# Head projections of a retention layer as one queued software pipeline of steps

## The chip, the cores and the metric

The kernel runs on one core of a Trainium2 chip. Five engines work side by side, each through its own queue of instructions in order: TensorE (PE, matrix multiplication, with a second row PEld for its weight loads), VectorE (DVE), ScalarE (ACT), GpSimd (POOL) and SyncE (SP), which here only issues transfers. Engines wait for each other through semaphores. Data lies in DRAM, in on-chip tiles of 128 partitions (SBUF), or in eight PSUM banks of 128 x 512 fp32, where TensorE adds up its products. The metric is the device time of one execution in microseconds, the median of the runs.

## What is computed

A trunk of two layers over 512 tokens of width 2048, in fp32. The first layer mixes tokens by retention with 8 heads, the second by latent attention with 16 heads; both are modulated by a vector `c` (shift, scale, gate).

```
for i in range(2):
    mod = (silu(c) @ ada_w[i] + ada_b[i])[:, None, :]     # ada_w[i]: 2048 x 6144
    shift, scale, gate = jnp.split(mod, 3, axis=-1)
    h = rmsnorm(x, norm_g[i]) * (1.0 + scale) + shift
    y = retention_branch(h, ...) if i == 0 else mla_branch(h, ...)
    x = x + gate * y
return rmsnorm(x, final_norm_g)

def retention_branch(h, pos, w_in, gn_g, w_out):
    proj = h @ w_in                                       # 2048 x 12288
    q, k, v, g = jnp.split(proj, [2048, 4096, 8192], axis=-1)
    q, k = rope(q, pos), rope(k, pos) / 16                # 8 heads of 256
    y = chunkwise_retention(q, k, v)                      # v, g: 8 heads of 512
    y = (y - mean(y)) * rsqrt(var(y) + EPS) * gn_g        # per head
    return (silu(g) * y) @ w_out
```

## The kernel before

*Numbers.* Matrices are kept as a high and a low half in TensorE's format fp32r, and each product is three matmuls (`mm3`, L158: high with high, high with low, low with high). A weight block arrives raw (fp32, 128 x 1024, 512 KB) through SP's queue, `load_w` (L138); `split` (L133) makes its halves: ACT copies the high half (L134), DVE subtracts to get the low one (L135). Raw tiles and halves rotate through three buffers each (tags `raw`, `whi`, `wlo`). Scratch tiles of 128 x 512 have the tag `tmp`, with six buffers. PSUM is two groups of four banks, `acc` and `aux`.

*Order.* The program is traced once in Python. A scheduler in the framework then sets the order on each engine, from its own estimate of when each instruction could start; `tc.issue_after(x)` tells it to place what is traced inside behind instruction x. DMA issues stand in the queue of the engine that issues them.

*Stages.* First the input is normalised and the first layer's modulation is computed from streamed rows (`first_modulation`), woven with head 0's q, k, v and most of its gates (0 to about 183 us); then the last gate block of head 0 (`g03`), and from 205 us head 1's queries and keys. The rotary tables `cos`, `sin` are made by `rotary_tables` with DVE in this first stage and stay on chip until the retention of the last heads.

The stage that the change rewrites runs over heads h = 1 to 7 (loop at its end):

- `queries_and_keys(h, ...)`, for h up to 5: eight units, each a weight block of two k-tiles, 24 matmuls of 128x128 by 128x512 (`qk_raw`, `qk_hi`, `qk_lo`); at the end the four banks are copied by ACT into `st` tiles and stored by POOL (`keep_rows`, L489).
- `values_and_gates(h)` (L603): v and g of a head with seven products in place of eight for each 2 x 2 block (a Strassen-Winograd form). `form_sums` makes the sums of the activations once, next to head 1's queries and keys. First half: eight units, each with two raw blocks e and o (`vg_e_w`, `vg_o_w`); DVE forms three sums of weights (L639 and the lines after it), both blocks are split (the low half at L627), and 24 matmuls go to the banks x, s, y, z. At the turn (L660 to L666) ACT copies x, s and z away to scratch (m1, m5, m4), and DVE adds m1 to y and y, m5 to s in PSUM. Second half: eight units of blocks p (128 x 1024) and q (128 x 512), one sum, both split (L671 for p's copy), 18 matmuls to x, y, s; the products of y and s are held one unit back at the start. At the end x and s go out by `keep_rows`, and m4 + y, m5 + y by DVE and POOL.
- Beside this the other modulation rows come in: six pieces of 16 rows of 512 KB, each row loaded by SP into `mod_aw` (two buffers, tag `bw`) and added by DVE into `mod_am` with a factor of `c` (`later_modulation`, L500, L512/L514). Two rows go with each unit of queries and keys from head 2 on, one with every other unit of the second half of values and gates (`qk_each`, `vg_each`). `use_modulation` (L519) sums a finished piece over the partitions with a few small matmuls and adds the bias; for a gate piece the bias is fetched by POOL into `mod_brow`, and the result is stored by POOL.

Then the tile pool `lp` is closed, and in the next one, `l1`, heads 6 and 7's queries and keys are computed, woven with the retention of heads 0 and 1 (`retention`, with `rope_halves` for the rotation); `hooks` says at which unit a generator of a head is advanced by one part. The part of a head before its first `yield` fetches and rotates q and k and fetches v; the next computes scores. Then follow the other heads' retention within the output projection (`o`), and the second layer.

Of the kernel before, what the change touches and what calls it, by code (L numbers as in the profile page):

```python
# [16 lines left out]
P = 128  # L17
# [32 lines left out]
def hybrid_trunk_kernel(  # L50
# [222 lines left out]
    def rot(name):  # L273
        return base.tile([P, T], F32, tag="rot", bufs=2, name=name)
# [81 lines left out]
    cos, sin = rot("cos"), rot("sin")  # L356
    tables = rotary_tables(cos, sin, 0, False, "ret")
# [98 lines left out]
    for u in range(KD // 2):  # L456
# [4 lines left out]
        if u + 1 < KD // 2:  # L461
            am = first_modulation(u + 1, (there, u))
        else:
            first_load(there, u)
            for _ in tables:
                pass
        for kind in (here, "g"):
            for kt in (2 * u, 2 * u + 1):
                in_order(lambda: products(kind, kt))
# [19 lines left out]
    def keep_rows(ps, dst_d, r0, name, func=AF.Identity, own=None):  # L489

        st = lpp.tile([P, T], F32, tag="st", bufs=4, name=name) if own is None else own(name)
        ACT.activation(st, ps, func)
        POOL.dma_start(dst_d[r0 : r0 + P, :], st)

    ripe = []
    clock = [0]

    def later_modulation(pool, pieces):  # L500
        for i, sect, part in pieces:
            name = f"mod_{i}_{sect}_{part}"
            c0 = sect * D + part * 1024
            am = pool.tile([P, 2, T], F32, tag="bm", bufs=2, name=f"{name}_am")
            for k in range(KD):
                aw = pool.tile([P, 2, T], F32, tag="bw", bufs=2, name=f"{name}_aw{k}")
                nc.sync.dma_start(
                    aw, (ada0, ada1)[i][:, k : k + 1, c0 : c0 + 1024].rearrange("p k (a n) -> p (k a) n", a=2)
                )
                ck = cact[:, k : k + 1]  # L510
                if k == 0:
                    DVE.tensor_scalar(out=am, in0=aw, scalar1=ck, scalar2=None, op0=ALU.mult)  # L512
                else:
                    DVE.scalar_tensor_tensor(out=am, in0=aw, scalar=ck, in1=am, op0=ALU.mult, op1=ALU.add)  # L514
                if k == KD - 1:
                    ripe.append((clock[0], name, i, sect, part, am))
                yield

    def use_modulation(age=2):  # L519

        clock[0] += 1
        while ripe and clock[0] - ripe[0][0] >= age:
            _, name, i, sect, part, am = ripe.pop(0)
            if sect < 2:
                ps = aux(f"{name}_ps")
                for b in range(8):
                    PE.matmul(
                        ps[:, b : b + 1], am[:, b // 4, b % 4 * P : (b % 4 + 1) * P], crow, start=True, stop=True
                    )
                mc = ps[:, 0:8]  # L530
                modulate(i, mc if sect == 0 else None, mc if sect == 1 else None, part * 8, 8)
                continue
            for j in range(2):
                ps = aux(f"{name}_ps{j}")
                n0 = part * 1024 + j * 512
                PE.matmul(ps, ones, am[:, j, :], start=True, stop=True)
                row = tmp(f"{name}_row{j}")
                brow = tmp(f"{name}_brow{j}")
                POOL.dma_start(brow[0:1, :], ada_b[i : i + 1, sect * D + n0 : sect * D + n0 + 512])
                DVE.tensor_add(row[0:1, :], ps[0:1, :], brow[0:1, :])  # L540
                POOL.dma_start(gate_d[i : i + 1, n0 : n0 + 512], row[0:1, :])

    later = later_modulation(lpp, [(i, s_, n) for i, s_ in ((0, 2), (1, 0), (1, 1)) for n in range(2)])

    def more(n=1):
        for _ in range(n):
            next(later, None)
# [14 lines left out]
    def form_sums(u):  # L562
# [3 lines left out]
        f = base.tile([P, 4, H], F32, tag="raw", bufs=3, name=f"sums_{u}_f")  # L566
# [18 lines left out]
    for b in range(4):  # L585
        keep_rows(qk0[b], qk_d, b * P, f"qk0_st{b}")
    for b in range(3):
        keep_rows(g0[b], g_d, b * P, f"g0_st{b}", AF.Silu, tmp)
    run(
        chunk(  # L590
            head_units(w_ret_in, 2, 8192 + 384, P, "g03", kn=8), [aux("g0_3")],
            lambda w, ki, kt, b: w_block(w, ki, b), lambda w, ki, kt, b: act_row(hT[kt]),
            lambda b, ps: keep_rows(ps, g_d, 3 * P, "g0_st3", AF.Silu),
        ),
        each=form_sums,
    )

    wvg = w_ret_in[:, 4096:12288].rearrange("k (j n) -> k j n", j=2)
# [4 lines left out]
    def values_and_gates(h):  # L603


        xb, sb = [acc(f"x{h}_{b}") for b in range(2)], [acc(f"s{h}_{b}") for b in range(2)]
        yb, zb = [aux(f"y{h}_{b}") for b in range(2)], [aux(f"z{h}_{b}") for b in range(2)]

        turn = [0]

        def load(src, name):

            n = turn[0] = turn[0] + 1
            shape = [P] + [d for d in src.shape[1:]]
            pool, tags = (lpp, ("own_r", "own_h", "own_l")) if n % 4 == 0 else (base, ("raw", "whi", "wlo"))
            raw, hi, lo = (
                pool.tile(shape, dt, tag=tag, bufs=1 if n % 4 == 0 else 3, name=f"{name}_{tag[-1]}")
                for tag, dt in zip(tags, (F32, F32R, F32R))
            )
            nc.sync.dma_start(raw, src)  # L620
            return raw, hi, lo
# [3 lines left out]

        def take_low(raw, hi, lo):
            DVE.tensor_sub(lo, raw, hi.bitcast(F32))  # L627
# [8 lines left out]
        for u in range(KD // 2):  # L636
            e, eh, el = load(block(2 * u, slice(0, 2)), f"vg{h}_{u}_e")
            o, oh, ol = load(block(2 * u + 1, slice(0, 2)), f"vg{h}_{u}_o")
            DVE.tensor_sub(e[:, 1, :], e[:, 1, :], e[:, 0, :])  # L639
            ACT.copy(eh, e)  # L640
            DVE.tensor_sub(o[:, 1, :], o[:, 1, :], e[:, 1, :])
            DVE.tensor_sub(o[:, 0, :], o[:, 0, :], o[:, 1, :])
            ACT.copy(oh, o)
            take_low(e, eh, el)
            take_low(o, oh, ol)
            b11, t1 = halves((eh, el), 2)
            t4, t2 = halves((oh, ol), 2)
            forms = [(xb, (0, 0), b11), (sb, 1, t1), (yb, 2, t2), (zb, (1, 1), t4)]
            if u == KD // 2 - 1:
                forms = [forms[i] for i in (0, 2, 1, 3)]  # L650
            for banks, n, w in forms:
                product(banks, n, u, w, u == 0)
            yield

# [6 lines left out]
        for b in range(2):  # L661
            DVE.tensor_add(yb[b], yb[b], m1[b])
        m5 = [put_by(sb[b], f"m5_{h}_{b}") for b in range(2)]
        for b in range(2):
            DVE.tensor_add(sb[b], yb[b], m5[b])
        m4 = [put_by(zb[b], f"m4_{h}_{b}") for b in range(2)]  # L666
        held = []
        for u in range(KD // 2):
# [14 lines left out]
            if u > 0:  # L683
                held = []
# [641 lines left out]
```

## Time and profile before

| | us |
|---|---|
| median of 3 runs (lowest, highest) | 2374.49 (2366.71, 2376.89) |
| the profiled execution | 2375.32 |
| its span in the trace | 2373.2 |
| mean granted TensorE clock, share of full | 0.976 |

The profile has a table of busy time for each engine, one of the span in 40 slices, the DMA queues, the chain of waits that ended last, groups of instructions by source line with the engine's idle time before them and what ended it, and the DMA issues with the median time from issue to landing. Names are those of the program with buffer numbers left out; a line may be that of a helper. In a table of waits the numbers are the total in us, the count, and the longest one; in a timeline, the start and the duration in us, the instruction, and in brackets the idle time before it with its releaser; in a table of windows, the length, then for PE, PEld, DVE, ACT and POOL the busy time with the number of instructions, the granted clock, the DMA engines' busy share and GB/s. DMA engines were busy through most of the span (tenths in 40 slices):

```profile
DMA  9965886776886565666555454555834333224533
q1 hardware_dynamic: 227872, 400.62, 53.5%
```

### The profile page before, as it was taken

The numbers are of one execution on the slowest core, as the hardware profiler recorded it, in microseconds if no ns is written. First come the engines' busy times: TensorE is split into PE (matmuls) and PEld (weight loads), VectorE is DVE, ScalarE is ACT, GpSimd is POOL, SyncE is SP. The second block draws the span as 40 slices with busy tenths as digits, with TensorE's granted clock in tenths as the row PEclk, the third lists the DMA queues.
The fourth block names the chain that finished last, engine by engine and source line by source line (L and its number), as shares of the span: only waits on it lengthen the run. The fifth ranks groups of instructions, "written<-read, shape, count | busy, mean of one in ns | idle before, by whom it ended". The sixth has DMA issues, their size and how long they took to land.

```text
span 2373.2 us, 28016 instructions
## 1 busy us (share of the span) xinstructions
PE 2229.5 (94%) x10186; PEld 1835.6 (77%) x10186; DVE 1508.6 (64%) x2247; ACT 1004.7 (42%) x1517; POOL 126.8 (5%) x228
## 2 busy tenths in 40 slices
PE   5998998898989989999899999998999999999997
PEld 4776776776868868778688888786778888888886
DVE  6888876767685566766565645447742257777545
ACT  5564332323233344433345554436232245555333
POOL 0000000010000000000000000010001000000000
PEclk9999999999999999999899999999999999999999
DMA  9965886776886565666555454555834333224533
GB/s 325 331 207 178 292 298 210 247 254 209 267 294 226 155 199 178 217 217 205 168 172 183 151 178 129 172 190 184 249 102 126 113 108 95 92 77 159 166 122 117
DMA packets 243114, 448.66 MB, mean 189 GB/s; under 512 B 21912, under 2 KB 95776, under 8 KB 242976
## 3 DMA queue, kind: packets, MB, share of 16 engines
q1 hardware_dynamic: 227872, 400.62, 53.5%
q0 software_dynamic: 14592, 46.18, 5.0%
q8 instruction: 79, 1.29, 0.2%
q14 instruction: 59, 0.48, 0.1%
q10 hardware_dynamic: 512, 0.08, 0.0%
HBM read 396.46 MB, written 50.35 MB: 188 GB/s over the span
## 4 chain that ended last, share of the span: by engine, by line
PE 47%; DMA 19%; DVE 17%; issue 10%; ACT 5%; POOL 1%; SPq 0%; DVEq 0%; ACTq 0%; POOLq 0%
PE o L160 4%; PE o L161 4%; PE o L162 4%; DMA mod_aw<-in_ada_w_dram 4%; DMA vg_e_w<-in_ret_w_in_dram 3%; DMA vg_o_w<-in_ret_w_in_dram 3%; PE g L160 2%; PE g L161 2%; PE g L162 2%; DMA aw<-in_ada_w_dram 2%; DVE mod_am L514 2%; DMA vg_q_w<-in_ret_w_in_dram 2%; PE qk L162 2%; PE qk L160 2%; PE qk L161 2%
## 5 line engine op out<-in xcount | busy, mean ns | idle before, releaser
L160 PE MATMUL o<-o_w_hi,o_h 128*128 128x512 f32 x768 | 301.9, 393 | 4.1 <-ACT o L912 3.6
L161 PE MATMUL o<-o_w_lo,o_h 128*128 128x512 f32 x768 | 299.6, 390 | 0.0
L162 PE MATMUL o<-o_w_hi,o_l 128*128 128x512 f32 x768 | 298.5, 390 | 0.0
L135 DVE TENSOR_TENSOR o_w_lo<-o_w_raw,o_w_hi 128x1024 fp32r<-128x1024 f32 x96 | 117.2, 1221 | 163.8 <-ACT o_w_hi L134 163.6
L514 DVE SCALAR_TENSOR_TENSOR mod_am<-mod_aw,cact,mod_am 128x1024 f32<-128x1024 f32 x120 | 153.7, 1281 | 47.5 <-DMA mod_aw<-in_ada_w_dram 46.7
L160 PE MATMUL qk<-hT,qk_hi 128*128 128x512 f32 x448 | 175.9, 393 | 1.7 <-ACT qk_hi L134 1.7
L162 PE MATMUL qk<-hT,qk_lo 128*128 128x512 f32 x448 | 173.8, 390 | 0.6 <-DVE qk_lo L135 0.6
L161 PE MATMUL qk<-hT,qk_hi 128*128 128x512 f32 x448 | 174.3, 389 | 0.0
L160 PEld LDWEIGHTS o<-o_w_hi,o_h 128*128 128x128 f32 x768 | 144.6, 188 | 37.1 <-ACT o L912 7.1
L162 PEld LDWEIGHTS o<-o_w_hi,o_l 128*128 128x128 f32 x768 | 144.2, 188 | 30.6 <-DVE o_l L135 0.6
L161 PEld LDWEIGHTS o<-o_w_lo,o_h 128*128 128x128 f32 x768 | 144.5, 188 | 29.0
L134 ACT CAST o_w_hi<-o_w_raw 128x1024 fp32r<-128x1024 f32 x96 | 101.0, 1054 | 118.1 <-PE o L162 90.6
L135 DVE TENSOR_TENSOR g_lo<-g_raw,g_hi 128x1024 fp32r<-128x1024 f32 (+1 forms) x42 | 49.2, 1172 | 114.8 <-ACT g_hi L134 101.9
L134 ACT CAST qk_hi<-qk_raw 128x1024 fp32r<-128x1024 f32 x64 | 67.3, 1051 | 126.2 <-PE qk L161 101.3
L135 DVE TENSOR_TENSOR qk_lo<-qk_raw,qk_hi 128x1024 fp32r<-128x1024 f32 x64 | 78.0, 1221 | 59.2 <-ACT qk_hi L134 50.2
L160 PE MATMUL g<-h,g_hi 128*128 128x512 f32 x256 | 100.6, 393 | 1.1 <-ACT ckv_n L1025 1.1
L135 DVE TENSOR_TENSOR o_l<-o_in,o_h 128x1024 fp32r<-128x1024 f32 x40 | 48.8, 1223 | 80.3 <-ACT o_h L134 80.3
L161 PE MATMUL g<-h,g_hi 128*128 128x512 f32 x256 | 99.6, 389 | 0.0
L162 PE MATMUL g<-h,g_lo 128*128 128x512 f32 x256 | 99.6, 389 | 0.0
L160 PEld LDWEIGHTS qk<-hT,qk_hi 128*128 128x128 f32 x448 | 84.1, 188 | 19.7 <-ACT qk_hi L134 2.3
L162 PEld LDWEIGHTS qk<-hT,qk_lo 128*128 128x128 f32 x448 | 84.0, 188 | 18.5 <-DVE qk_lo L135 1.0
L161 PEld LDWEIGHTS qk<-hT,qk_hi 128*128 128x128 f32 x448 | 84.1, 188 | 17.8 <-issue 0.5
(450 smaller groups left out, 5461.9 us busy)
## 6 DMA issues: line engine op xcount, KB each, us to landing
mod_aw<-in_ada_w_dram SPq DMA_DIRECT2D x128, 512.0 KB, 4.7
aw<-in_ada_w_dram SPq DMA_DIRECT2D x128, 256.0 KB, 6.0
qk_raw<-in_ret_w_in_dram SPq DMA_DIRECT2D x128, 256.0 KB, 4.5
o_w_raw<-in_ret_w_out_dram SPq DMA_DIRECT2D x64, 512.0 KB, 3.8
vg_e_w<-in_ret_w_in_dram SPq DMA_DIRECT2D x56, 512.0 KB, 4.5
vg_p_w<-in_ret_w_in_dram SPq DMA_DIRECT2D x56, 512.0 KB, 3.9
g_raw<-in_mla_w_in_dram SPq DMA_DIRECT2D x32, 512.0 KB, 3.7
o_w_raw<-in_mla_w_out_dram SPq DMA_DIRECT2D x32, 512.0 KB, 3.8
```

The source lines that it names most:

```text
L134: ACT.copy(hi, src)
L135: DVE.tensor_sub(lo, src, hi.bitcast(F32))
L160: PE.matmul(o, lhs[0], rhs[0], start=first and not seeded, stop=False, skip_group_check=seeded)
L161: PE.matmul(o, lhs[0], rhs[1], start=False, stop=False, skip_group_check=seeded)
L162: return PE.matmul(o, lhs[1], rhs[0], start=False, stop=last, skip_group_check=seeded)
L514: DVE.scalar_tensor_tensor(out=am, in0=aw, scalar=ck, in1=am, op0=ALU.mult, op1=ALU.add)
```

## The change

1. **Steps.** Head 0's `g03`, the queries and keys of heads 1 to 5, and the values and gates of heads 1 to 7 become one list of `Step` objects, each with `load`, `prepare` (combine and split), `multiply` and `follow` (what comes after the last matmul: evacuation, additions in PSUM). The loop issues step i+2's load, step i+1's prepare, the modulation work of step i, step i+1's modulation row fetches, step i's matmuls, and its follow. Each part is traced inside `behind(...)`, which places it after the last instruction so far on the named engines, so on SP, DVE, ACT and PE the scheduler keeps the traced order. POOL is not named.
2. **Buffers.** Raw tiles of values and gates alternate between `raw` (3) and `own_r`, which has 3 buffers now and 1 before; the halves take the `own_h`/`own_l` pair every fourth time. `st` has 2 buffers and had 4 (every other evacuation uses `tmp` instead), and the rotary tables are no longer in the pool `base`.
3. **Rotary tables.** They are made in pool `l0p` in the last unit of head 0's stage, stored to DRAM (`tables_d`) by POOL, and fetched again by SP when `l1` opens. The second layer's pair comes from its own pool.
4. **Modulation.** `later_modulation` yields each addition as a function, so a row's fetch and its addition are queued at different places: fetched in step i, added in step i+1. `use_modulation` is divided: `sum_modulation` puts the small matmuls behind a step (only steps with `banks_free`, u < 5 of queries and keys), and `use_modulation` takes the results in the next one. Row counts: two for each step of queries and keys in heads 2 to 5; in the second half of values and gates one in each odd step, and for heads 6 and 7 one in each but the first.
5. **Order inside values and gates.** A step of the first half goes x, s, z, y and went x, s, y, z; its last one goes x, y, s, z in both. In the second half each step goes x, y, s (no holding back), and the last x, s, y. `form_sums` of head 1 is spread over six of its eight steps, into `own_r`, and two run in the two steps of `g03`.
6. **After the stage.** In `retention` the fetch and split of v move behind the scores. Head 1's parts are advanced at units 3 and 7 of head 6's and 1 and 3 of head 7's queries and keys (before: 5, then 1, 3, 5). Head 7's evacuation goes to tiles with the tag `yn` instead of `tmp`. In the second layer `g2_each` queues the remaining gate rows with `behind`.

```diff
+    class Step:
+        def __init__(self, load, prepare, multiply, follow=None, rows=0, sums=None, banks_free=False):
...
+    def plain_steps(nu, kn, parts, cn, name, take, n, lhs, rhs, evac, **kw):
...
+            def load():
+                w["raw"] = base.tile([P, kn, cn], F32, tag="raw", bufs=3, name=f"{name}_{u}_r")
...
+            def prepare():
...
+                split(w["raw"], *w["hl"])
...
+    def raw_tile(shape, name):
+        turn[0] += 1
+        if turn[0] % 2:
+            return base.tile(shape, F32, tag="raw", bufs=3, name=f"{name}_r")
+        return lpp.tile(shape, F32, tag="own_r", bufs=3, name=f"{name}_r")
+    def part_tiles(shape, name):
+        turn[1] += 1
+        pool, tags, n = (lpp, ("own_h", "own_l"), 1) if turn[1] % 4 == 0 else (base, ("whi", "wlo"), 3)
+        return [pool.tile(shape, F32R, tag=tag, bufs=n, name=f"{name}_{tag[-2]}") for tag in tags]
+    def seven_steps(h):
...
+            def prepare():
+                e, o = w["e"], w["o"]
+                if not second:
+                    eh, el = part_tiles([P, 2, T], f"{n}e")
+                    DVE.tensor_sub(e[:, 1, :], e[:, 1, :], e[:, 0, :])
+                    ACT.copy(eh, e)
+                    DVE.tensor_sub(o[:, 1, :], o[:, 1, :], e[:, 1, :])
+                    DVE.tensor_sub(o[:, 0, :], o[:, 0, :], o[:, 1, :])
+                    DVE.tensor_sub(el, e, eh.bitcast(F32))
+                    oh, ol = part_tiles([P, 2, T], f"{n}o")
+                    ACT.copy(oh, o)
+                    DVE.tensor_sub(ol, o, oh.bitcast(F32))
...
+            def follow():
+                if not second and u == KD // 2 - 1:
+                    m1[:] = [put_by(x_[b], f"m1_{h}_{b}") for b in range(2)]
+                    for b in range(2):
+                        DVE.tensor_add(y_[b], y_[b], m1[b])
+                    m5[:] = [put_by(s_[b], f"m5_{h}_{b}") for b in range(2)]
+                    for b in range(2):
+                        DVE.tensor_add(s_[b], y_[b], m5[b])
+                if second and u == 0:
+                    m4[:] = [put_by(z_[b], f"m4_{h}_{b}") for b in range(2)]
...
+            return Step(load, prepare, multiply, follow, rows=int(second and (u % 2 == 1 or (h > 5 and u > 0))))
...
+                rows=lambda u, h=h: 0 if h == 1 else 2,
+                sums=lambda u, h=h: {0: 2, 1: 3, 3: 4, 4: 5, 6: 6, 7: 7}.get(u) if h == 1 else None,
+                banks_free=lambda u: u < 5,
...
+    @contextmanager
+    def behind(*engines):
+        with ExitStack() as stack:
+            for e in engines:
+                ins = next((i for i in reversed(nc.cur_bb.bb.instructions) if i.engine == e), None)
+                if ins is not None:
+                    stack.enter_context(tc.issue_after(ins))
+            yield
...
+    for i, step in enumerate(steps):
+        if i + 2 < len(steps):
+            with behind(E_.SP):
+                steps[i + 2].load()
+        if i + 1 < len(steps):
+            with behind(E_.DVE, E_.Activation):
+                steps[i + 1].prepare()
+        with behind(E_.DVE, E_.Activation):
+            use_modulation()
+            for add in fetched:
+                add()
+            fetched = []
+            if step.sums is not None:
+                form_sums(step.sums)
+        if i + 1 < len(steps):
+            for _ in range(steps[i + 1].rows):
+                with behind(E_.SP):
+                    fetched += [f for f in (next(later, None),) if f is not None]
+        with behind(E_.PE):
+            step.multiply()
+            if step.banks_free:
+                sum_modulation()
+        with behind(E_.DVE, E_.Activation):
+            step.follow()
...
+    cos, sin = rot(l1p, "cos"), rot(l1p, "sin")
+    for n, t in enumerate((cos, sin)):
+        nc.sync.dma_start(t, tables_d[n * P : (n + 1) * P, :])
...
-        (6, {0: r_[:1], 3: r_[:1], 5: r_, 7: r_[:1]}),
-        (7, {1: r_[1:], 3: r_[1:], 5: r_[1:]}),
+        (6, {0: r_[:1], 3: r_, 5: r_[:1], 7: r_}),
+        (7, {1: r_[1:], 3: r_[1:]}),
```

368 lines of the change are left out of this document (194 added, 174 removed).

## The prediction

> **What bounds the kernel now.** I read the page's busy table first, then one window over the stage that the change rewrites (249 us, where head 1's values and gates start, to 1048 us), then TensorE's waits inside it.
>
> ```profile
> span 2373.2 us, 28016 instructions
> PE 2229.5 (94%) x10186; PEld 1835.6 (77%) x10186; DVE 1508.6 (64%) x2247; ACT 1004.7 (42%) x1517; POOL 126.8 (5%) x228
> 249.00:1048.00 799.00, 746.92 (x3195) 604.13 (x3194) 552.39 (x629) 291.19 (x357) 42.57 (x81) 0.97 0.71 231
> PE x L633 <- DVE vg_p_o L627: 24.1, 9, 4.6
> PE x L633 <- DVE vg_e_o L627: 16.7, 8, 6.2
> PE y L633 <- DVE vg_o_l L627: 4.9, 5, 1.4
> PE y L632 <- DVE s L665: 3.1, 1, 3.1
> PE x L632 <- ACT qk_st L492: 2.4, 2, 2.2
> ```
>
> TensorE is the bound, yet in this stage it waits 51.5 us in all (the five waits and a sixth of 0.3), nearly always for VectorE (DVE) to finish the low half of a weight block, though DVE is busy only 552 of 799 us. So the order of DVE's work is at fault, not its amount. What the waits cost beyond themselves, and the pace of an undisturbed TensorE, stand in its timeline:
>
> ```profile
> 301.35 0.79 PE L632 MATMUL y<-vg_q_i,sums 128*128 128x512 f32 x1 [3.06 <-DVE s L665]
> 303.66 0.63 PE L634 MATMUL x<-vg_p_i,hT 128*128 128x512 f32 x1
> 307.50 0.63 PE L633 MATMUL s<-vg_p_o,sums 128*128 128x512 f32 x1
> 309.21 0.40 PE L633 MATMUL y<-vg_q_l,sums 128*128 128x512 f32 x1
> 313.30 0.39 PE L633 MATMUL y<-vg_q_o,sums 128*128 128x512 f32 x1
> ```
>
> Eighteen matmuls from 309.21 to 313.30 go at 0.227 us each; the nine after 303.66, behind a gap of 3.06, at 0.427. One long gap thus costs about 2 us more. The stage holds 7 x 336 + 4 x 192 = 3120 matmuls, or 709 us at 0.227. Of the 90 us above that, 51.5 are waits, about 18 (nine long gaps at 2) is the slow pace behind them, and some 20 are left: the small modulation sums on TensorE and short irregularities, which I keep.
>
> **The change, part by part.** *Steps.* A step (one weight block or pair) is loaded two steps ahead and split one step ahead; DVE and ScalarE (ACT) take splitting, modulation and evacuation in that fixed order. A step of `qk`, and one of the first half of values and gates, is 24 matmuls, 5.45 us; one of the second half is 18, 4.09 us. DVE's and ACT's work for one:
>
> ```profile
> L514 DVE SCALAR_TENSOR_TENSOR mod_am<-mod_aw,cact,mod_am 128x1024 f32<-128x1024 f32 x85 | 108.9, 1281 | 28.6 <-DMA mod_aw<-in_ada_w_dram 28.1
> L627 DVE TENSOR_TENSOR vg_p_o<-vg_p_w,vg_p_i 128x1024 fp32r<-128x1024 f32 x56 | 68.3, 1221 | 29.7 <-ACT vg_p_i L671 29.5
> L135 DVE TENSOR_TENSOR qk_lo<-qk_raw,qk_hi 128x1024 fp32r<-128x1024 f32 x34 | 41.4, 1222 | 34.3 <-ACT qk_hi L134 29.5 <-PE mod_ps L536 4.2 <-DMA qk_raw<-in_ret_w_in_dram 0.6
> L639 DVE TENSOR_TENSOR vg_e_w<-vg_e_w 128x512 f32<-128x512 f32 x54 | 37.0, 687 | 34.0 <-DMA vg_e_w<-in_ret_w_in_dram 33.7
> L671 ACT CAST vg_p_i<-vg_p_w 128x1024 fp32r<-128x1024 f32 x56 | 58.8, 1050 | 81.7 <-PE y L634 73.9 <-DMA vg_p_w<-in_ret_w_in_dram 4.1 <-PE s L634 3.5
> ```
>
> First half: 3 x 0.69 + 2 x 1.22 = 4.5 us on DVE, below 5.45. Second half: 0.69 + 1.22 + 0.69 = 2.6, with one modulation row 3.9, below 4.09. Six raw buffers let a load start a step before it is needed. The split tiles come free when the step before last ends on TensorE; the copy (1.05) and the subtraction (1.22) then take 2.3 us of the 4.09. So inside both halves no wait is left. At the turn between the halves, where the longest vg_p_o waits lie, the split of the first p and q is now queued ahead of the four combination adds (0.69 each); those fit beside the end of TensorE's last first-half step, in which x and y are finished before s and z, and beside the next step's products of x. At a head's end z is now used before y, so y's four adds are covered by the 18 matmuls ahead of it. The 70 us go; bounds are 51 (the waits alone) and 75.
>
> *What comes in their place: the modulation rows.* In the `qk` steps of heads 2 to 5 two rows per step are fetched into two buffers, and each fetch waits for the add that frees its buffer. Before, the same pattern ran freely here:
>
> ```profile
> 346.59 1.28 DVE L514 SCALAR_TENSOR_TENSOR mod_am<-mod_aw,cact,mod_am 128x1024 f32<-128x1024 f32 x1 [5.16 <-DMA mod_aw<-in_ada_w_dram]
> 349.01 1.28 DVE L514 SCALAR_TENSOR_TENSOR mod_am<-mod_aw,cact,mod_am 128x1024 f32<-128x1024 f32 x1 [1.13 <-DMA mod_aw<-in_ada_w_dram]
> 352.47 1.28 DVE L514 SCALAR_TENSOR_TENSOR mod_am<-mod_aw,cact,mod_am 128x1024 f32<-128x1024 f32 x1 [1.04 <-DMA mod_aw<-in_ada_w_dram]
> 355.30 1.28 DVE L514 SCALAR_TENSOR_TENSOR mod_am<-mod_aw,cact,mod_am 128x1024 f32<-128x1024 f32 x1 [1.55 <-DMA mod_aw<-in_ada_w_dram]
> 358.59 1.28 DVE L514 SCALAR_TENSOR_TENSOR mod_am<-mod_aw,cact,mod_am 128x1024 f32<-128x1024 f32 x1 [0.87 <-DMA mod_aw<-in_ada_w_dram]
> mod_aw<-in_ada_w_dram SPq DMA_DIRECT2D x5, 512.0 KB, 4.7
> mod_brow<-in_ada_b_dram POOLq DMA_DIRECT2D x1, 2.0 KB, 8.2
> ```
>
> A pair comes round in (358.59 - 346.59)/2 = 6.0 us: 4.7 of landing and 1.28 of add. TensorE needs a step every 5.45. In DVE's queue the next subtraction now stands behind the adds, so DVE falls back 0.55 us a step, 4.4 a head. SyncE's (SP's) queue has the same chain: the weight load behind two waiting fetches starts only after the second add. At the end of `qk` the first two steps of values and gates need 4.5 + 2.6 us of DVE while rows are still added, against 5.45: 1.6 us each. With 1 us of lead at the start that is 4.4 + 3.2 - 1 = 6.6 us a head, 26 for four heads. Below, 0: rows landing faster, or the lead of two steps swallowing it. Above, 45: rows landing in 6 us (pair 7.3 us).
>
> *Sums on TensorE.* They are now queued right behind a `qk` step. Counting rows (4 in head 1, then 20 a head, 16 to a piece), two pieces are complete inside head 3 (step 3) and head 4 (step 1), so TensorE waits for adds of that very step, 2 to 5 us; that lets DVE catch up, so I add 3 us for both. The first gate sum also needs `brow` (landing 8.2): DVE would stand until some 16 us into head 3, within what step 3 allows; nothing. Half pace behind new stalls: 3 us. New stalls together 32 us (0 to 60).
>
> By the Trainium skill, "DMA: Bandwidth & Descriptors", section "Anatomy of one DMA" (measured on the software path), a transfer takes 2.0 us plus its bytes at 436 GB/s, 3.2 us for 512 KB; no run here shows that for this loaded queue, the row has 4.7, and the row decides. By that rule a pair would come round in 4.5 us and the 26 us would be nothing (second case below).
>
> *Start, tables, end.* The tables' two stores to DRAM are short, but at the start ACT evacuates `qk0` bank 1 into a tile over the tables' old place, hence waits for those stores, and head 0's last gate block is split behind it in ACT's queue. Rows around it:
>
> ```profile
> 182.58 0.68 DVE L301 SCALAR_TENSOR_TENSOR cos<-sin 128x512 f32<-128x512 f32 x1
> 188.34 1.04 ACT L134 CAST g_hi<-g_raw 128x1024 fp32r<-128x1024 f32 x1 [3.51 <-DMA g_raw<-in_ret_w_in_dram]
> 205.32 0.50 PE L160 MATMUL qk<-hT,qk_hi 128*128 128x512 f32 x1 [1.67 <-ACT qk_hi L134]
> g_d<-g_st POOLq DMA_DIRECT2D x4, 256.0 KB, 7.3
> ```
>
> Tables done by about 182, two issues, 5.5 to 7.3 us of landing: the block is split at about 190 instead of 188.3, 1.5 us lost, against 1.7 won at 205. Net 0 (-4 to +2). The six `form_sums` in head 1 now share DVE with one subtraction a step, about 5.3 us, covered.
>
> ```profile
> 1057.00 0.69 DVE L738 TENSOR_TENSOR rope_t<-qk,cos 128x512 f32<-128x512 f32 x1 [1.56 <-DMA qk<-qk_d]
> 1065.93 0.50 PE L160 MATMUL s<-qk_0p,qk_0p 128*128 128x512 f32 x1 [1.33 <-ACT qk_0p L134]
> 1164.68 0.69 DVE L740 TENSOR_TENSOR rope_t<-qk,sin 128x512 f32<-128x512 f32 x1 [4.41 <-issue]
> 1172.77 0.79 PE L160 MATMUL s<-qk_0p,qk_0p 128*128 128x512 f32 x1 [10.38 <-ACT qk_0p L134]
> ```
>
> After the stage, cos and sin are fetched ahead of head 0's queries: about 1 us later, as much as the second sum on TensorE covers. The gap of 10.38 comes from head 2's rotation waiting for scratch that holds `qk7`; those now go to other tiles, head 1 runs two units earlier, and in the new order 72 matmuls of the output projection (16 us) stand ahead of head 2's scores. 10.4 and 2.5 of slow pace go: 13 (0 to 14). The later gate rows are queued differently in a stretch without waits: nothing.
>
> **Sum.** 70 - 32 + 0 + 13 = 51 us gained. The profiled execution took 2375.3 us (span 2373.2), within 1 us of the median 2374.5, so 2375 - 51 = 2324.
>
> **The rivals.** *Rows come round fast enough, or the lead holds* (19%): 26 us less of stalls, about 2297. For it: qk_raw and mod_aw land in as little as 2.9 and 3.5 us; against: 4.7 in the very place. *Only half the waits go* (11%): new coupling in head 3 and at the turns, 2350. *The waits move to buffers* (7%): `st` has two tiles instead of four, and evacuations at 14 chunk ends hold ACT, with the next split behind them, until stores land. With
>
> ```profile
> v_d<-m POOLq DMA_DIRECT2D x1, 256.0 KB, 8.7
> ```
>
> and some 5 us of cover, 14 x 4 = 56 us: no gain, 2375. Against: a tile's last store is a chunk, 44 us or more, old. *The row fetches starve the weight loads* (11%), the slower one: in the 32 `qk` steps with rows a load is issued after step k's adds, lands, is copied (1.05), subtracted (1.22), and two adds (2.6) follow, two steps on: (landing + 6)/2 a step. At 4.7 that is 5.4, harmless; it decides from 6.0, and loses more than the forecast's gain at about 9.4 (7.7 a step). At 10.2, the longest landing of a row, 8.1 x 32 against 6.0 x 32 is 67 us more: 2389.
>
> ```profile
> DMA to landing us min/median/max: 3.5/4.7/10.2
> DMA to landing us min/median/max: 2.9/4.6/8.8
> ```
>
> (rows, then `qk` blocks; the maxima are single loads.)
>
> **How the numbers follow.** Forecast 52%, 2305 to 2340; the rivals hold 19, 11, 7 and 11. A change within 0.5% (12 us) can't be told from none: faster 0.52 + 0.19 + 0.11 = 0.82, same 0.07, slower 0.11. The range 2290 to 2355 takes in the fast rival and the half gain and leaves out no gain and loss.
>
> **What would show it.** Right: in the after profile the waits of x on the low halves at the turns are gone; the stage from head 1 to 7 lasts about 760 us instead of 799; what is left of TensorE's waits sits in `qk` steps of heads 2 to 5 and just behind them, on low halves standing behind mod_am adds, and at a modulation sum in heads 3 and 4; no 10 us gap ahead of head 2's scores. Wrong: waits at every chunk end on ACT for stores, or weight loads landing late in `qk`.

## The result, and the profile after

The changed kernel takes 2290.61 us (median of 4 runs, 2288.54 to 2291.51) against 2375.69 us for the kernel before (2366.71 to 2379.84): ratio 0.9646, 95% interval 0.9617 to 0.9674, a gain of 85 us. Forecast were 2324 us, a gain of 51. The page of the changed kernel begins:

```profile
span 2288.5 us, 28030 instructions
PE 2204.8 (96%) x10186; PEld 1830.2 (80%) x10186; DVE 1517.9 (66%) x2239; ACT 1008.0 (44%) x1515; POOL 127.5 (6%) x230
```

DVE, ACT and POOL are busy as long as before or a little longer. TensorE runs the same 10186 matmuls in 25 us less of busy time (2229.5 before), as fewer of them go at the slow pace behind a gap; the rest of the 85 us is idle time that has gone. The stage of heads 1 to 7, and what TensorE waits for in it (the table of windows and the table of waits, changed kernel):

```profile
247.50:989.90 742.40, 728.56 (x3193) 598.81 (x3192) 572.68 (x638) 303.26 (x362) 44.39 (x83) 0.99 0.76 254
```

```profile
PE x L607 <- ACT qk_st L494: 6.8, 2, 4.2
PE mod_ps L755 <- DVE mod_am L742: 3.5, 1, 3.5
PE mod_ps L762 <- DVE mod_am L742: 2.5, 1, 2.5
PE x L608 <- DVE vg_01e_l L639: 0.5, 1, 0.5
```

TensorE's waits in the stage fell from 51.5 to 13.3 us. Of those on low halves 0.5 us is left; the others are on evacuations (`qk_st`) and on additions of rows that a modulation sum needs (`mod_ps`). By stretches, cut at first or last matmuls of the same groups in TensorE's timeline (the last column is the best kernel of the experiments below):

| stretch, us | before | changed | best |
|---|---|---|---|
| start to head 1's values and gates | 249.0 | 247.5 | 239.1 |
| heads 1 to 7 | 798.5 | 742.4 | 722.2 |
| q and k of heads 6 and 7, first retention, to the o matmuls at 1271.7 (before) | 224.2 | 211.8 | 212.7 |
| output projection with the rest of retention | 331.4 | 331.7 | 331.0 |
| h2, cq, ckv of the second layer | 135.9 | 121.6 | 121.5 |
| rest | 634.2 | 633.5 | 633.4 |
| span | 2373.2 | 2288.5 | 2259.9 |

So 56.1 us come from the stage that was rewritten, 12.4 from the gap ahead of head 2's scores, and 14.3 from a stretch to which the prediction had given nothing. The start moves by some 5 us from one traced run to the next, so its 1.5 says little.

### The profile page after: what moved, and what is told of

The parts are those of the page before. It is cut to its first block, busy times and chain, and to the rows that moved or that the text cites. A ratio compares the mean times of both kernels' runs of the same rounds, so it can differ in the third digit from the quotient of the medians.

```text
span 2288.5 us, 28030 instructions
## 1 busy us (share of the span) xinstructions
PE 2204.8 (96%) x10186; PEld 1830.2 (80%) x10186; DVE 1517.9 (66%) x2239; ACT 1008.0 (44%) x1515; POOL 127.5 (6%) x230
## 4 chain that ended last, share of the span: by engine, by line
PE 48%; issue 29%; DMA 8%; DVE 8%; ACT 5%; POOL 1%; SPq 0%; ACTq 0%; POOLq 0%; DVEq 0%
PE o L160 5%; PE o L162 5%; PE o L161 5%; PE g L160 3%; PE g L162 3%; PE g L161 3%; DMA aw<-in_ada_w_dram 2%; DVE am L398 2%; DMA mod_aw<-in_ada_w_dram 2%; PE qk L162 1%; PE qk L161 1%; PE qk L160 1%; DMA o_in<-y_d 1%; ACT p L1268 1%; PE pT L1281 1%
## 5 line engine op out<-in xcount | busy, mean ns | idle before, releaser
L742 DVE SCALAR_TENSOR_TENSOR mod_am<-mod_aw,cact,mod_am 128x1024 f32<-128x1024 f32 x120 | 153.7, 1281 | 24.6 <-DMA mod_aw<-in_ada_w_dram 23.8
L160 PE MATMUL qk<-hT,qk_h 128*128 128x512 f32 x320 | 126.5, 395 | 0.0
L162 PE MATMUL qk<-hT,qk_l 128*128 128x512 f32 x320 | 125.4, 392 | 0.3
L161 PE MATMUL qk<-hT,qk_h 128*128 128x512 f32 x320 | 125.1, 391 | 0.0
L134 ACT CAST qk_h<-qk_r 128x1024 fp32r<-128x1024 f32 x40 | 41.8, 1048 | 124.6 <-DMA qk_r<-in_ret_w_in_dram 116.6
L398 DVE SCALAR_TENSOR_TENSOR am<-aw,cact,am 128x512 f32<-128x512 f32 x120 | 90.1, 751 | 3.6
L134 ACT CAST g_hi<-g_raw 128x1024 fp32r<-128x1024 f32 (+1 forms) x40 | 40.4, 1009 | 113.9 <-PE g L161 105.9
L135 DVE TENSOR_TENSOR qk_l<-qk_r,qk_h 128x1024 fp32r<-128x1024 f32 x40 | 48.9, 1225 | 48.4 <-ACT qk_h L134 48.4
L134 ACT CAST o_h<-o_in 128x1024 fp32r<-128x1024 f32 x40 | 42.0, 1053 | 83.4 <-PE o L161 60.8
```

What stands on the lines that cost most here:

```text
L134: ACT.copy(hi, src)
L135: DVE.tensor_sub(lo, src, hi.bitcast(F32))
L160: PE.matmul(o, lhs[0], rhs[0], start=first and not seeded, stop=False, skip_group_check=seeded)
L161: PE.matmul(o, lhs[0], rhs[1], start=False, stop=False, skip_group_check=seeded)
L162: return PE.matmul(o, lhs[1], rhs[0], start=False, stop=last, skip_group_check=seeded)
L398: DVE.scalar_tensor_tensor(out=am, in0=aw[:, j], scalar=ck, in1=am, op0=ALU.mult, op1=ALU.add)
```

## The experiments

A total without a range or a ratio below is that of a single execution.

### What the second layer's stretch gained from

The windows of this stretch, first before, then changed:

```profile
1603.10:1739.00 135.90, 120.76 (x536) 96.51 (x535) 98.00 (x141) 59.46 (x108) 8.91 (x14) 0.95 0.66 203
1533.40:1655.00 121.60, 116.67 (x537) 95.85 (x536) 64.49 (x112) 59.49 (x108) 8.39 (x14) 0.97 0.35 107
```

The columns after PE and PEld show it: DVE had 98.0 us of work there and now has 64.5. A timeline of DVE in the kernel before names the work that is gone:

```profile
1629.21 0.54 DVE L982 TENSOR_SCALAR h2f<-x1T,a_col,b_col 128x256 f32<-128x256 f32 x1
1629.67 1.28 DVE L514 SCALAR_TENSOR_TENSOR mod_am<-mod_aw,cact,mod_am 128x1024 f32<-128x1024 f32 x1
1630.86 0.75 DVE L983 TENSOR_TENSOR h<-h2f,h 128x256 fp32r<-128x256 f32 x2
```

The gate rows of the second layer stood between the pieces of h2, for which TensorE was waiting. Its two largest waits in this stretch of the kernel before (13.8 us in all there, 5.0 in the changed kernel):

```profile
PE x1T L965 <- DVE h2f L982: 4.8, 3, 4.3
PE ckv L160 <- ACT cq_n L1025: 4.2, 2, 2.2
```

Traced in the gate loop that follows, the rows had been pulled forward by the scheduler, whose order took them as free to go. The views of the tile `mod_am` give where 30 of its 32 additions lie, before and changed:

```profile
L514 DVE SCALAR_TENSOR_TENSOR mod_am<-mod_aw,cact,mod_am x30: 1274/1283/1287, 1629.7 to 1726.6; 128x1024 f32<-128x1024 f32 x30
```

```profile
L742 DVE SCALAR_TENSOR_TENSOR mod_am<-mod_aw,cact,mod_am x30: 1264/1279/1285, 1648.7 to 1802.3; 128x1024 f32<-128x1024 f32 x30
```

Two kernels test it from both sides. The first ties the rows' fetches and additions in the kernel before, and takes over nothing else of the change:

```diff
-            use_modulation()
-            more()
+            with behind(E_.DVE, E_.SP):
+                use_modulation()
+                more()
```

> The kernel before with one part of the change alone: in the gate loop of the second layer each row's fetch and addition is queued behind what stands so far on DVE and SP. Theory A (14.3 of the 85 us come from the second layer's gate rows, which the scheduler had pulled forward among the h2 and ckv work): the stretch from the last o matmul to the first g matmul, 135.9 us before (39.6 and 96.3), falls to about 122; total about 2361 us. Rival B (that stretch is faster in the changed kernel only because it begins 70 us earlier and meets other transfers): it stays at 136, total about 2375.

The second takes the ties out of the changed kernel's `g2_each` (all three calls stand free).

> The changed kernel with the second layer's gate rows left to the scheduler again. Theory A: mod_am additions come back among the h2 and ckv work, the stretch of 121.6 us (32.3 and 89.3) grows to about 136, total about 2305 us. Rival B: 122 and 2291 us.

The windows of the stretch, held in the kernel before and then free in the changed one, and the former's largest wait after the gate loop:

```profile
1608.30:1731.00 122.70, 116.00 (x538) 94.44 (x536) 61.91 (x109) 59.26 (x108) 8.32 (x14) 0.99 0.32 97
```

```profile
PE mod_ps L536 <- DVE mod_am L514: 30.5, 2, 25.5
```

```profile
1539.00:1674.30 135.30, 119.46 (x538) 95.53 (x536) 97.95 (x142) 60.04 (x108) 9.17 (x14) 0.96 0.66 206
```

In the stretch theory A holds on both sides: 122.7 with the rows held, 135.3 with them free. The free one takes 2309.7 us in all (A: 2305). The held one missed its total: 2397.98 us (median of 4), ratio 1.0089 (1.0056 to 1.0122), 0.9% slower than before. Its rows began only at 1871 us, and TensorE waited 30.5 us for the last of them ahead of the attention. That fits a tie which gives an earliest place and no latest one, since all untied work stays free to go ahead; it was not tested. (Within one tied part the scheduler's order is free too: in the changed kernel three matmuls of z start at 247.52, ahead of the first of x at 248.47, which was traced first.) The changed kernel also ties the sums on TensorE and adds each row one unit after its fetch. Which of the two keeps its rows in pace was not tried.

### Does the fixed order do it, or the new steps?

In the changed kernel's loop `behind(...)` is replaced by an empty context, first for all engines, then only where it names DVE and ACT. Steps, buffers and traced order stay.

> The changed kernel with the same steps, buffers and traced order in the stage of heads 1 to 7, but none of it tied to a queue: the scheduler orders all engines. Theory C (the fixed order is what removes the waits of x on the low halves): those waits come back, the stage of 742.4 us grows to 780 or more, total 2325 or more. Rival D (the two-step lead, the six raw buffers and the new order of products do it): the stage stays below 750, total below 2300.

> As the run before, but TensorE and SP keep the traced order and only DVE and ACT are left to the scheduler. If DVE's and ACT's order is the part of theory C that counts, the stage is about as long as with nothing tied (780 or more); if SP's order of loads against row fetches is, it stays near 742 and the wait of x at 373 us (4.2, on the evacuation) may go, as ACT may then evacuate ahead of the copy: 738 to 745.

The stage with nothing tied and its largest waits, then with only TensorE and SP tied:

```profile
237.60:1004.60 767.00, 736.39 (x3194) 601.06 (x3192) 552.44 (x626) 298.71 (x357) 43.42 (x82) 0.98 0.75 243
```

```profile
PE y L607 <- DVE s L678: 11.7, 6, 3.2
PE x L608 <- DVE vg_01e_l L639: 7.6, 4, 3.4
PE z L608 <- DVE vg_00o_l L642: 7.3, 2, 5.8
```

```profile
250.20:1031.10 780.90, 741.04 (x3193) 602.35 (x3192) 556.60 (x627) 299.26 (x357) 43.50 (x82) 0.98 0.73 240
```

```profile
PE y L607 <- DVE s L678: 13.5, 7, 3.4
PE s L607 <- ACT qk_st L494: 10.8, 4, 3.8
```

Neither theory took it all. Of the 56.1 us, 31.5 (798.5 to 767.0) come without any tie, and 24.6 need the ties: without them the combination adds at the turn (L678) and the first low halves of a head stand too late in DVE's order. What gave the 31.5, the traced order, the lead of two steps, the buffers or the order of the products, was not taken apart. Half the ties are worse than none: 780.9. The figure was expected, but only because nothing tied was expected at 780 too. TensorE waits there for evacuations that the free ACT order puts late: in head 2 a copy for the next step, at 381.39 after 3.42 us of idle time, goes ahead of the third evacuation at 382.34. The untied kernel's total was 2306.8 us, against 2325 or more in C and under 2300 in D.

### The stalls that are left: two waits, one cause

The changed kernel's first long wait, from TensorE's timeline, and ACT's around it:

```profile
373.24 0.80 PE L607 MATMUL x<-vg_00e_h,hT 128*128 128x512 f32 x1 [4.25 <-ACT qk_st L494]
```

```profile
368.51 1.05 ACT L636 CAST vg_00e_h<-vg_00e_r 128x1024 fp32r<-128x1024 f32 x1 [6.23 <-DVE vg_00e_r L635]
371.65 1.04 ACT L641 CAST vg_00o_h<-vg_00o_r 128x1024 fp32r<-128x1024 f32 x1 [2.09 <-DVE vg_00o_r L638]
372.60 2.05 ACT L494 ACTIVATE qk_st<-qk 128x512 f32<-128x512 f32 x4
```

ACT is idle, yet evacuates head 2's banks only at 372.60: the copies of the next step stand ahead in its queue, and these wait for weights that came late. SP's queue shows why they are late. The load of `vg_00e` stands behind two row fetches, and what row fetches wait for here is the addition that frees their buffer (SP's table of waits from 316 to 372 us, then its timeline):

```profile
SPq L733 <- DVE mod_am L742: 29.0, 14, 6.3
```

```profile
359.82 1.66 SPq L733 DMA_DIRECT2D mod_aw<-in_ada_w_dram  x2
361.58 0.39 SPq L628 DMA_DIRECT2D vg_00e_r<-in_ret_w_in_dram  x1
```

Is that a cost of its own beside the two waits at `mod_ps`? One kernel sums each finished piece one step later (`due = len(ripe)` is taken before the step's additions, and `sum_modulation(due)` sums no more than that):

> The changed kernel with a finished modulation piece summed on TensorE one step after the step that adds its last row, so that no matmul waits for an addition of its own step. Theory E (TensorE's 6.0 us of waits at mod_ps and the slow pace behind them are a loss of their own): heads 3 and 4's queries and keys fall from 51.6 and 52.4 us to about 46.5 each, nothing is given back, total about 2280 us. Rival F (row fetches go a little slower than a step, and those waits only let DVE and SP catch up): the queries and keys fall to about 46.5, but x of heads 3 and 4's values and gates then waits for the evacuation as in head 2 (up to 7 us each), total 2286 to 2294 us.

Stage and largest wait:

```profile
242.10:984.70 742.60, 727.53 (x3193) 596.97 (x3192) 572.67 (x638) 302.74 (x362) 44.19 (x83) 0.99 0.76 254
```

```profile
PE x L607 <- ACT qk_st L494: 11.2, 4, 4.4
```

The waits at `mod_ps` are gone, and the stage is as long as before, 742.6 against 742.4: now four heads wait for their evacuation instead of two. Rival F is right. (The total, 2284.9, is lower by the earlier start of this run, whose stage begins at 242.1 instead of 247.5 us.) Another kernel goes for the cause:

```diff
-                aw = pool.tile([P, 2, T], F32, tag="bw", bufs=2, name=f"{name}_aw{k}")
+                aw = pool.tile([P, 2, T], F32, tag="bw", bufs=3 if pool is lpp else 2, name=f"{name}_aw{k}")
...
-        return lpp.tile(shape, F32, tag="own_r", bufs=3, name=f"{name}_r")
+        return lpp.tile(shape, F32, tag="own_r", bufs=2, name=f"{name}_r")
```

> The changed kernel with three buffers for modulation rows in place of two (and two own_r buffers in place of three, which pays for it). Theory F' (a row's fetch waits for the addition that frees its buffer, and the weight loads behind it in SP's queue come late: that makes the waits of x on qk_st at 373 and 756 us, 6.8 us, 10.3 with the slow pace behind them): both go, total about 2280 us. Rival G (the DMA engines, busy at 0.76 of the stage, set how fast rows come): rows land later instead, the waits stay, total about 2290 us.

Its stage, then the low halves of head 2's blocks (`qk_l`: count, ns, first and last start) and the landing of the rows beside them, in the changed kernel and in this one:

```profile
245.10:966.50 721.40, 720.66 (x3193) 594.97 (x3193) 571.70 (x638) 303.28 (x362) 44.25 (x83) 1.00 0.78 262
```

```profile
L135 DVE TENSOR_TENSOR qk_l<-qk_r,qk_h x8: 1224/1226/1227, 320.0 to 362.3; 128x1024 fp32r<-128x1024 f32 x8
```

```profile
DMA to landing us min/median/max: 3.2/4.4/5.8
```

```profile
L135 DVE TENSOR_TENSOR qk_l<-qk_r,qk_h x8: 1220/1225/1226, 317.6 to 355.2; 128x1024 fp32r<-128x1024 f32 x8
```

```profile
DMA to landing us min/median/max: 3.4/5.4/6.6
```

With two row buffers a step of DVE takes (362.3 - 320.0)/7 = 6.0 us, with three (355.2 - 317.6)/7 = 5.4, and TensorE needs 5.45. Rows land later with three (5.4 against 4.4 us), but they are asked for earlier, so rival G falls. The total is 2270.2 us, ten below theory F', since the waits at `mod_ps` had the same cause and went too (0.2 us left). TensorE is busy for 720.7 of 721.4 us, at a granted clock of 1.00.

By the Trainium skill, "Perfetto Trace Analysis", section "Optimization Strategy", a gap that recurs through a stretch on the engine that should be full can mean too few buffers for the next tile. The trace agrees as far as one buffer more ended the recurring gaps and took 21.0 us off the stage; but the tile that lacked it is none that TensorE waits for directly.

The same buffer in the kernel before, paid for with two `st` tiles in place of four:

> The kernel before with three buffers for modulation rows and two st tiles in place of four, in the scheduler's own order. Theory M (a third row buffer pays where the loads stand behind row fetches in a fixed order, so it is a cure for the new order and not for the old one, whose waits come from the place of DVE's low halves): the stage of 798.5 us stays within 792 to 805 and the total within 2366 to 2385. Rival N (row fetches hold SP's queue in the old order too): the stage falls by 10 us or more, total 2364 or less.

Its stage, TensorE's largest wait and a wait of ACT:

```profile
250.70:1049.50 798.80, 749.01 (x3194) 607.50 (x3193) 553.41 (x627) 294.74 (x355) 43.00 (x80) 0.97 0.70 230
```

```profile
PE s L632 <- ACT qk_st L492: 20.0, 9, 5.1
```

```profile
ACT qk_st L492 <- DMA qk_d<-qk_st: 25.6, 9, 6.8
```

The stage is 798.8 us and the total 2377.33 us (median of 8), ratio 1.0014 (0.9988 to 1.004), as in theory M, but that doesn't settle it: the waits on `vg_e_o` (16.7) went, and evacuations that wait for stores out of the two `st` tiles came. What a third row buffer alone would do in the old order stays open.

### Six raw buffers, and the tables' trip to DRAM

Four raw buffers (own_r every fourth time, one buffer), and the tables kept on chip with five:

> The changed kernel with four raw buffers for values and gates (three raw, one own_r, every fourth in own_r) in place of six, and a tile of its own for the sums of form_sums. The prediction's step (six raw buffers let a load start a step before it is needed, and that is part of why no wait is left inside the halves): waits of vg tiles on loads or low halves come back, 0.3 us or more in most of the 112 steps, the stage at 760 or more instead of 742, total 2308 or more. Rival J (a load has a step of 4.1 to 5.5 us and lands in about 4.6; four are enough when the order is fixed): 742 to 748, total below 2297.

> The changed kernel with the rotary tables kept on chip: no stores to DRAM, no fetch at the l1 stage, and two own_r buffers in place of three (five raw buffers in all), which pays for it. The prediction's term (the trip to DRAM costs nothing net, -4 to +2): the gap ahead of g at the start shrinks by 1 to 2 us since no evacuation waits for the stores; l1's first scores come within 1 us; the stage stays at 742 (740 to 748); total 2288 to 2296. Rival L (the sixth raw buffer is what the tables were moved for and it pays): the stage grows by 5 us or more.

The stage with four, with a wait of the kind that came back, and the stage with five:

```profile
244.00:995.60 751.60, 729.91 (x3193) 596.68 (x3192) 574.09 (x638) 301.16 (x362) 44.03 (x83) 0.99 0.76 251
```

```profile
PE x L608 <- DVE vg_15o_l L649: 4.1, 6, 1.3
```

```profile
236.30:984.60 748.30, 729.87 (x3193) 599.80 (x3192) 573.07 (x638) 303.37 (x362) 44.73 (x84) 0.98 0.77 253
```

Four buffers cost 9.2 us, five 5.9: a modest price. With four the stage lies between the two forecasts (760 or more, 748 or less); with five, rival L's growth of 5 us or more is met. And the five of the kernel with three row buffers can cost 0.7 us at most, as TensorE is busy for all but that of its 721.4. This fits a sixth buffer that covers loads standing behind row fetches and isn't needed with the fetches in time; six with three row buffers were not run.

At the start the kernel with the tables on chip has no gap ahead of head 0's last gate block at all. In the changed kernel it is 5.48 us. The wait that the prediction named is there, but it is the smaller part: ACT stands idle for 1.09 us at an evacuation, for the tables' stores by the view of `tables_d`. The rest is ACT's order, in which the block's copy stands behind the tables' sine and cosine and the evacuations. ACT in the changed kernel, then with the tables kept:

```profile
188.72 1.09 ACT L494 ACTIVATE qk_st<-qk 128x512 f32<-128x512 f32 x2 [1.09 <-issue]
189.69 1.99 ACT L134 CAST g_h<-g_r 128x1024 fp32r<-128x1024 f32 x2
```

```profile
174.07 1.07 ACT L134 CAST g_h<-g_r 128x1024 fp32r<-128x1024 f32 x1
```

With the tables kept the scheduler puts the copy 15.6 us earlier, ahead of all these, and TensorE never waits for it, where 1 to 2 us less of gap were expected. So this kernel changes ACT's order along with the stores, and what the trip alone costs stays open. The total, 2285.6 us, is just below the 2288 to 2296 expected: the stage begins 11.2 us earlier, of which some 5 may be the moving start, and is 5.9 us longer.

### The gap ahead of head 2's scores

Two kernels undo one part each of the changed l1 stage: head 7's evacuation back in `tmp`; or the old units for head 1 and v ahead of the scores, with the evacuation left in `yn`.

> The changed kernel with head 7's queries and keys evacuated to the scratch tiles (tmp) again, the rest as changed. Theory H, that of the prediction (the 10.38 us ahead of head 2's scores came from its rotation waiting for scratch that held qk7): the stretch of 211.8 us from the first matmul of head 6 to the o matmuls that follow head 2 grows by 8 to 13 us, total 2299 to 2304. Rival I (the earlier parts of head 1 and the later v, which put 72 o matmuls ahead of those scores, cover it alone): 212, total 2291.

> The changed kernel with head 1's retention advanced at the old units and v fetched and split ahead of the scores again, while head 7's evacuation stays in the yn tiles. Theory H (the scratch tiles alone made the gap of 10.38 us): the stretch from head 6's first matmul to the o matmuls after head 2 stays at 212 to 214 us, total about 2292. The prediction's wording (the earlier head 1 and 72 o matmuls ahead of the scores are part of it): 216 to 224 us, total 2295 to 2303.

The stretch with `tmp` and its gap in the timeline, then the stretch with the old units:

```profile
988.40:1213.00 224.60, 212.69 (x977) 177.02 (x978) 135.88 (x225) 88.23 (x130) 15.12 (x24) 0.97 0.57 186
```

```profile
1115.24 0.80 PE L160 MATMUL s<-qk_0p,qk_0p 128*128 128x512 f32 x1 [10.40 <-ACT qk_0p L134]
```

```profile
991.00:1202.00 211.00, 208.54 (x979) 174.02 (x978) 138.22 (x229) 90.29 (x134) 15.64 (x25) 1.00 0.63 203
```

The scratch tiles are the whole of it, 12.8 us. Head 1's earlier units and v's later place, undone together, gain nothing here (211.0 against 211.8). Totals 2303.2 and 2292.2, as theory H had them.

### A kernel that beats both

Three row buffers, and at the start the evacuations of head 0 queued on ACT behind the copy of the last gate block:

```diff
     steps[0].prepare()
-    for b in range(4):
-        keep_rows(qk0[b], qk_d, b * P, f"qk0_st{b}", own=in_turn(b))
-    for b in range(3):
-        keep_rows(g0[b], g_d, b * P, f"g0_st{b}", AF.Silu, tmp)
+    with behind(E_.Activation):
+        keep_qk0(0, 2)
+        for b in range(3):
+            keep_rows(g0[b], g_d, b * P, f"g0_st{b}", AF.Silu, tmp)
...
                 steps[i + 1].prepare()
+        if i == 0:
+            with behind(E_.Activation):
+                keep_qk0(1, 3)
```

> The kernel with three row buffers, and at the start head 0's evacuations queued on ACT behind the copy of head 0's last gate block, those into st tiles behind the second one. Theory K (the gap of 5.5 us ahead of the g matmuls at 190.8 is ACT standing at qk_st for the tables' stores, with that copy behind it): the copy starts at about 185.6, after the tables' sine and cosine, in place of 189.7; the gap shrinks to 1 to 2 us and its slow pace goes, 5 us in all; total about 2265 us against 2291 for the changed kernel. Rival: the evacuations that now stand later hold back head 1's queries and keys, and the gain is given back there, total about 2270.

TensorE's first matmul on head 0's last gate block:

```profile
182.13 0.50 PE L160 MATMUL g<-hT,g_h 128*128 128x512 f32 x1 [1.36 <-ACT g_h L134]
```

It takes 2261.82 us (median of 5, 2258.26 to 2263.58), ratio 0.9522 (0.9509 to 0.9535) to the kernel before: 29 us better than the changed kernel, 20.2 of them in the stage and 8.4 at the start, of which some 5 may be the moving start. Theory K's gap of 1 to 2 us is there at 1.36: the copy begins 0.3 us after TensorE's last product before it (at 181.05), against 4.4 in the changed kernel, though the trip of the tables is kept. The slow pace did not go, though (last section). Head 1's queries and keys aren't held back (43.7 us in both).

## Why the prediction was right, and where it fell short

The direction was right, and in the main for the reasons given; the time was 34 us below the forecast, outside the forecast's own range of 2305 to 2340 and close to the fast rival's 2297. That it lies inside the wide range, which starts at 2290, is luck: by 0.6 us. Of the 34 us, 14.3 came from a stretch priced at nothing, 11 from stalls priced too high, 7 from waits priced too low and 1.5 from the start. Step by step:

- *Waits of the stage removed: 70 foreseen, 77 measured* (798.5 to the 721.4 of the kernel without new stalls). Right, a little low. That nothing would be left inside the halves and at the turns held. The reason given first, the fixed order, is not all of it: the same steps without ties gave 31.5 of the 56.1 us net.
- *New stalls: 32 foreseen, 21.0 measured* (742.4 to 721.4). The place and the mechanism were right, and so was the pace: 6.0 us a pair of rows in head 2, as foreseen. By the rule of the Trainium skill ("DMA: Bandwidth & Descriptors", section "Anatomy of one DMA") the estimate would have been 4.5 and free; the measurement sides with the row. What failed is the size of two terms. The waits, rows (26) and sums (3), came to 13.3 us: each of the four heads lost 2.5 to 4.3 in one long wait where 6.6 was foreseen. In head 2 the wait of 4.25 is about the lag of 4.4 from the eight steps; the 1.6 at each of two steps behind them did not come on top. The wait at a sum was no term of its own either, but the same stall at another place: DVE and SP catch up in it, and the head's end is spared. Later sums showed it, with nothing gained. The other 7.7 us, by difference, are the slow pace behind the gaps, put at 3. Also the stall came out not as 1.6 us of low halves at two steps but as ACT's evacuation, queued behind the copies of late weights; that was not foreseen.
- *Start: 0 foreseen, 1.5 gained.* The copy came at 189.7, foreseen 190, but by luck: the tables were done at 185.7 and not at 182, and their stores landed in 2.3 and 2.6 us and not in 5.5 to 7.3. The named wait was 1.1 us; most of the gap came from ACT's order, which the prediction did not weigh.
- *Gap ahead of head 2's scores: 13 foreseen, 12.4 measured.* Of the three reasons given only the scratch tiles count.
- *Later gate rows: "queued differently in a stretch without waits: nothing"; 14.3 measured.* This is the step that failed outright. The stretch from 1603 to 1739 had waits, of h2, ckv and kr, and they were not traced to the rows that stood among them. To look at where the kernel before really ran those 32 additions would have shown it.
- *The rivals.* The fast one was nearest in time, but by another road: neither did the rows come round fast enough, nor did the lead of two steps hold. Evacuations that wait for stores out of two `st` tiles did not show in the changed kernel; in the old order they do (25.6 us). The starving of weight loads by row fetches, whose late landing was named as a sign of being wrong, exists, at 21 us for the stage rather than at a loss.
- *Prices that do not follow from their own terms.* None of them moves the forecast. Rows landing in 6 us give 16.8 us a head by the prediction's sum, 67 in all and not 45. In the slower rival the copy, the subtraction and two adds are 4.9 us and not 6, and 67 us more is 2391 and not 2389. Half of the waits gone would be 2359 and not 2350, 56 us of waits for stores 2380 and not 2375.

## What to carry to other kernels

A list scheduler may pull side work forward into a stretch where its engine sets the end: look for where each group really ran, not for where it is written, before a tie on it is priced at nothing. When order is fixed, queue heads decide: a fetch that waits for its buffer delays every load behind it, so try one buffer more for the side stream than it seems to need (here one buffer of rows was worth 21 us, and a sixth weight buffer could have added 0.7 at most after that). Stalls that come from one late chain should not be added up: here the chain's lag came out once a head, at a sum or at the head's end.

## What was not expected of the hardware

In head 2's queries and keys the median landing of a 512 KB row rose from 4.4 to 5.4 us with three buffers, while the pair's round fell from 6.0 to 5.4 us: the landing time of one transfer was no measure of the stream. And a whole stage of 3193 matmul records ran at 720.7 busy of 721.4 us with a granted clock of 1.00, against 0.97 before: with the gaps, the slow pace behind them is gone as well.

Short gaps in a row can cost more than a longer one alone. The best kernel's start just behind the gap of 1.36 us shown above, then the changed kernel's second wait at an evacuation, both from TensorE's timeline:

```profile
183.39 0.57 PE L162 MATMUL g<-hT,g_l 128*128 128x512 f32 x1 [0.53 <-DVE g_l L135]
183.76 0.63 PE L160 MATMUL g<-hT,g_h 128*128 128x512 f32 x1
...
186.74 0.56 PE L161 MATMUL g<-hT,g_h 128*128 128x512 f32 x1
```

```profile
756.58 0.50 PE L607 MATMUL x<-vg_00e_h,hT 128*128 128x512 f32 x1 [2.59 <-ACT qk_st L494]
756.92 0.40 PE L608 MATMUL x<-vg_00e_l,hT 128*128 128x512 f32 x1
```

Behind gaps of 1.36 and 0.53 us the matmuls from 183.76 to 186.74 take 0.43 us each, at a granted clock of 0.54 (183.4 to 187.1 us); behind a single one of 2.59 the pace is full at once, with 1.00 (756.5 to 761). The prediction's own case of slow pace, at 303.66, also stands behind two gaps, of 3.06 and 0.93 us (at 303.07). By the Trainium skill, "TensorE: Matmul & The Clock Gate", section "Why this matters for your kernels", gaps above some 3 us bring the slow clock back. The second case agrees, the first does not: 1.9 us in two pieces were enough there. Why was not tested.
